# A gated-DeltaNet layer with SwiGLU: TensorE in order of emission in two phases, and transpositions in runs of eight

## The chip, the cores and the metric

One core of a Trainium2 chip runs the kernel. The metric is the device time of one execution in microseconds (us). TensorE is PE in the profile, and its weight loads are PEld; VectorE is DVE, ScalarE is ACT, GpSimd is POOL, and SyncE (SP) issues most of the transfers.

## The reference, cut to what matters

One decoder layer, 256 tokens wide, model width 2048, all in float32:

```python
mod = (silu(c) @ mod_w + mod_b)                  # 6 rows of 2048: sh1 sc1 ga1 sh2 sc2 ga2
h = x * (1 + sc1) + sh1
qkv, z, b, a = split(h @ w_in)                   # 2048 -> 8192 + 4096 + 64
qkv = silu(causal_depthwise_conv(qkv, conv_w))   # 4 taps
q, k = l2norm per head; beta = sigmoid(b); g = -exp(a_log) * softplus(a + dt_bias)
# chunked delta rule: (L + I) is unit lower triangular, L = strict(kb @ k.T) * decay
u, w = solve(L + I, [v * beta, kb * exp(gc)]); o, state = scan over chunks
y = (o * rsqrt(mean(o*o) + eps) * norm_w * silu(z)) @ w_out
x = layer_norm(ALPHA * x + (1 + ga1) * y)
h = x * (1 + sc2) + sh2
y = (silu(h @ w_gate) * (h @ w_up)) @ w_down     # 2048 -> 2 * 5632 -> 2048
out = layer_norm(ALPHA * x + (1 + ga2) * y)
```

## The kernel before, in words

Every weight matrix is streamed once in tiles of 128 x 1024 (`load_split`, L182 to L192: two tiles of 128 rows by 512 columns). ACT rounds a tile to `wh` (L190), and DVE takes the rest, `wl` (L191); a product of full precision is then three products, `wh` with the high half of the activations, `wl` with it, and `wh` with the low half (`Group.product`, L223 to L225). A `Group` makes 512 columns of output for both halves of the tokens: a chunk of 4 row blocks is 4 x 2 x 3 = 24 products of 512 columns, and one `wl` serves 12 of them. Four buffers each hold `raw`, `wh` and `wl`.

**The planner.** The program is unrolled by Python. `pos` counts chunks: one unit of position is 24 products. `Group.chunk` calls `advance(n + i/8)` ahead of every three products, and this runs each task that is due (`spawn(t, generator)`); a task that yields `d` goes on `d` units later. `at(p)` gives what is emitted a priority, the smaller the earlier. The order of each engine's instructions is then settled by the scheduler of the framework, engine by engine: from what is ready in its own model of time it takes the smallest priority. So positions decide priorities, and the order of TensorE is not that of the emission.

**Phase 1** (L924 to L935) makes the input projections for four groups of heads, `q` = 0 to 3, and the eight groups of the gate z (`z_group`). The groups of q = 0, and keys and queries of q = 1, are made ahead of it in parts. Behind a finished group come tasks. `conv_silu` (L457) turns two heads (`tr`, L462, four transpositions), convolves them on DVE (`cy`, L470, six a pair) and yields SILU units; then they are turned back (L494, L529). CONV is the distance of the first turn from its group. `gdn(q)` (L691) starts at some position s. Its four `la_task`s begin at s, s+0.5, s+1 and s+1.5 (LAGAP); each turns `dg` after LA1 (L547) and multiplies keys and queries after LA2 more (L556), and DVE writes `LA`. At s+3.0 `solve_task` (L564) is emitted, which inverts the 32 x 32 blocks on DVE: a transposition into `LD` (L573), 31 dependent pairs of `tmp` (L584) and `X` (L586), and a transposition into `XD` (L588). SOLVE = 5.4 units later (for q = 3 another ALONE = 1.5) TensorE's small products with `XD` follow (L600, L601), then four more steps, each HOP units on, and `state_task`. `gdn(q+1)` waits for the end of `gdn(q)`.

`mods_late` (L326) makes the rows ga1, sc2 and sh2 beside this: 32 loads a row, each with one accumulation `macc` on DVE (L272). At the end of half a row TensorE sums over partitions in four products (L351), ACT copies the sums (L277), and TensorE turns the copy (`to_columns`, L280) in the same step, with no yield between. Each of these float32 products stands twice in the trace.

**Phase 2** multiplies by `w_out` and takes the first layer norm; **phase 3** (L1046 to L1055) makes 11 gate and 11 up groups of 512 columns and then the down product. After an up group `act_task` turns 2 x 4 tiles of `an` = silu(gate) * up (L1039; `an` is L1031) and splits them (L814, L815); before, its two keys are due 0 and 0.5 units after the group's end. ga2's two halves are made in phase 3 as above, one `macc` every 2 units.

Of the kernel before, what the change touches and what calls it, by code (L numbers as in the profile page):

```python
# [2 lines left out]

# [6 lines left out]
F32R = mybir.dt.float32r  # L10
# [8 lines left out]
KT = D // 128  # L19
FF = 5632  # L20
FT = FF // 128
NQ = 4
# [7 lines left out]
def gdn_layer_kernel(ctx: ExitStack, tc: tile.TileContext, x, c, mod_w, mod_b, ln_g, ln_b,  # L30
# [3 lines left out]

    SPLIT, MOD0, MODEVERY = 10, 30.0, 0.95
    MGAP, CGAP0, CGAP, CSTEP = 1.5, 1.0, 2.0, 2.3
    CONV, PAIR, SILU = 0.2, 0.4, 2.4
    GDN, LAGAP, LA1, LA2, LA3, SOLVE, HOP = 3.0, 0.5, 0.3, 0.6, 1.5, 5.4, 0.6
    ALONE, MACW, ZW, OW = 1.5, 1.0, 0.1, 0.3


# [3 lines left out]
    held = ctx.enter_context(tc.tile_pool(name="held", bufs=1))  # L45
# [22 lines left out]
    def spawn(t, gen):  # L68
        heappush(tasks, (t, len(seq), gen))
        seq.append(gen)  # L70
# [3 lines left out]
    def drain(but=None):  # L74
        while any(x_[2] is not but for x_ in tasks):
            advance(now[0] + 0.1)

    def advance(t):
        now[0] = t
        while tasks and tasks[0][0] <= t:  # L80
            t0, i, gen = heappop(tasks)
            with at(t0):
                d = next(gen, None)
            if d is not None:
                heappush(tasks, (t0 + d, i, gen))
# [4 lines left out]
    def tp():  # L90
        return psum.tile([128, 512], F32, name="tp", tag="tp", bufs=2)
# [10 lines left out]
    w_in2 = w_in.rearrange("l k n -> (l k) n")  # L102
    w_out2 = w_out.rearrange("l k n -> (l k) n")
    w_gu2 = w_gu.rearrange("l k n -> (l k) n")
# [72 lines left out]
    pos = [0]  # L177
# [299 lines left out]
    def evac(t, ps):  # L477
        n = gp.tile([128, 512], F32, name="nat", tag="nat", bufs=4)
        act(n, ps, AF.Copy)
        return n  # L480
# [243 lines left out]
    def conv_start():  # L724
        t = max(now[0] + CONV, conv_free[0])
        conv_free[0] = t + CSTEP
        return t

    def qk_done(q, which):
        nat = []  # L730

        def done(t, ps, n=None):
            nat.append(evac(t, ps) if n is None else n)
            if t == 0:
                return
            both = []
            ss = work.tile([128, 2, 4], F32, name="ss", tag="ss", bufs=2)
            t1 = conv_start()
            for h in (0, 2):
                spawn(t1 + PAIR / 2 * h, qk_pair(q, which, nat, h, ss, both))  # L740
            spawn(t1 + PAIR + SILU + 0.6, qk_norm(q, which, ss, both))
        return done

    def v_done(q, half):
        nat = []

        def done(t, ps, n=None):
            nat.append(evac(t, ps) if n is None else n)
            if t == 0:
                return  # L750
            if q not in oq:
                oq[q] = held.tile([128, 2, 8, 128], F32, name=f"oq{q}", tag=f"o{q}")
            t1 = conv_start()
            for h in (0, 2):
                spawn(t1 + PAIR / 2 * h, v_pair(q, half, nat, h))
            if half == 1:
                spawn(t1 - CONV + GDN, gdn(q))
        return done
# [149 lines left out]
    def late_mods():  # L908
        yield from mods_late(ga1, 32, 1.0, MODEVERY)
        yield from mods_late(sc2, 64, 1.0, MODEVERY)  # L910
        yield from mods_late(sh2, 48, 0.0, MODEVERY)
        tt(A2, lng[:, 0:KT], sc2, op=OP.mult)
        tt(B2, lnb[:, 0:KT], sc2, op=OP.mult)
        tt(B2, B2, sh2, op=OP.add)
# [3 lines left out]
    mods_gen = late_mods()  # L918
    spawn(MOD0, mods_gen)

    def z_group(q, half):
        Group(w_in2, 8192 + q * 1024 + half * 512, h_hi, h_lo, KT, z_done(q, half)).run()

    for q in range(1, NQ):  # L924
        if q > 1:
            Group(w_in2, 2048 + q * 512, h_hi, h_lo, KT, qk_done(q, 0)).run()
            Group(w_in2, q * 512, h_hi, h_lo, KT, qk_done(q, 1)).run()
        for half in range(2):
            Group(w_in2, 4096 + q * 1024 + half * 512, h_hi, h_lo, KT, v_done(q, half)).run()
        if q == 1:  # L930
            z_group(0, 0)
    for z in range(1, 2 * NQ):
        z_group(z // 2, z % 2)
    z1 = pos[0]
    drain(mods_gen)  # L935

    with at(z1 - 2):
        r = [held.tile([128, D], F32, name=f"r{t}", tag=f"h{t}") for t in range(2)]
# [55 lines left out]
    NACT, NLATE = 13, 19  # L994
# [16 lines left out]
    late = {}  # L1011
# [7 lines left out]
    with tc.tile_pool(name="ph3", bufs=1, reuse_waits="tile") as p3:  # L1019
        def gate_done(j):  # L1020
            def done(t, ps):
                gates_[j, t] = p3.tile([128, 512], F32, name="sg", tag="sg", bufs=2)
                act(gates_[j, t], ps, AF.Silu)
            return done

        nats = {}

        def up_done(j):
            def done(t, ps):
                nats[j, t] = p3.tile([128, 512], F32, name="an", tag="an", bufs=6)  # L1030
                tt(nats[j, t], ps, gates_[j, t], op=OP.mult)  # L1031
            return done

        def act_task(key):
            j, i2 = divmod(key, 2)
            p = tp()
            for i in range(2):
                for t in range(2):
                    tr(p[:, i * 256 + t * 128:i * 256 + (t + 1) * 128],  # L1039
                       nats[j, t][:, (2 * i2 + i) * 128:(2 * i2 + i + 1) * 128], ident)  # L1040
            aT[key] = late[key] if key >= NACT else pair_tiles(p3, f"aT{key}")
            split_into(*aT[key], p)
            return
            yield

        for j in range(11):  # L1046
            Group(w_gu2, j * 512, h2_hi, h2_lo, KT, gate_done(j)).run(8 if j == 0 else 4, 8 if j == 0 else 4)
            Group(w_gu2, FF + j * 512, h2_hi, h2_lo, KT, up_done(j)).run()
            if j == 10:
                lt = [held.tile([128, 8, 256], F32R, name=f"lt{i}", tag=f"o{i}") for i in range(2)]  # L1050
                for i in range(22 - NLATE):
                    late[NLATE + i] = (lt[0][:, 2 * i:2 * i + 2, :], lt[1][:, 2 * i:2 * i + 2, :])
            for key in (2 * j, 2 * j + 1):
                if key < NLATE:
                    spawn(pos[0] + 0.5 * (key % 2), act_task(key))  # L1055
        drain()
        with at(pos[0]):
            for key in range(NLATE, 22):
                for _ in act_task(key):
                    pass  # L1060
        row2 = gate_row("h3", ga2, "ga2row")
        r2 = [held.tile([128, D], F32, name=f"rr{t}", tag=f"o{2 + t}") for t in range(2)]
        for t in range(2):
            nc.gpsimd.dma_start(r2[t], x1s[t])


        lrow = {}

        def finish(t):

            with at(now[0] - 40):
                mean, rstd, shift = norm_scalars(st2, t)

            shares = ((0, 0, 512, True), (1, 0, 512, True), (2, 0, 512, False), (3, 0, 512, False)) if t == 0 else (
                (0, 0, 512, True), (1, 0, 512, True), (3, 0, 512, False), (2, 0, 256, True), (2, 256, 512, False))
            for g, c0, c1, by_dve in shares:
                ot = r2[t][:, g * 512 + c0:g * 512 + c1]
                gamma, bias = (lrow[i, g][:, c0:c1] for i in range(2))
                if by_dve:
                    stt(ot, ot, mean, gamma, op0=OP.subtract, op1=OP.mult)  # L1080
                    stt(ot, ot, rstd, bias, op0=OP.mult, op1=OP.add)
                else:
                    act(ot, ot, AF.Identity, scale=rstd, bias=shift)
                    nc.gpsimd.tensor_tensor(ot, ot, gamma, op=OP.mult)
                    nc.gpsimd.tensor_tensor(ot, ot, bias, op=OP.add)
                nc.sync.dma_start(out2[t * 128:(t + 1) * 128, g * 512 + c0:g * 512 + c1], ot)

        def down_done(g):
            def done(t, ps):
                with at(now[0] - (40 if g == 3 else 0)):  # L1090
                    residual(row2, g, t, ps, r2, st2)
                if g == 3:
                    finish(t)
            return done

        for g in range(4):
            if g == 1:
                for i, src in enumerate((ln_g, ln_b)):
                    for gg in range(4):
                        tag, n = ("sg", 2) if i and gg > 1 else ("an", 6)  # L1100
                        lrow[i, gg] = p3.tile([128, 512], F32, name=f"l{i}{gg}", tag=tag, bufs=n)
                        nc.gpsimd.dma_start(lrow[i, gg], src[:, 1, gg * 512:(gg + 1) * 512].to_broadcast([128, 512]))
            Group(w_down2, g * 512, *pair_of(aT), FT, down_done(g)).run(8 if g == 3 else 4)
# [29 lines left out]
```

## Time and profile before

| | |
|---|---|
| median of 3 runs | 1722.5 us (1720.7 to 1725.71) |
| the profiled execution | 1725.16 us, of it 1723.4 us the span of its instructions |
| PE busy | 1668.0 us (97%), 8685 products |
| DVE busy | 1139.7 us (66%) |
| ACT busy | 882.0 us (51%) |
| HBM | 226 GB/s over the span |

Phase 1's groups stand from about 217 to 790 us, phase 2 to 967 us, the gate and up groups to 1470 us, and the down product to the end. PE's busy time is a union in which pipelined products overlap. So costs are read from starts: what separates the starts of two products beyond their usual distance is the cost of what stands between them.

### The profile page before, as it was taken

What the parts mean: (1) busy time and instruction counts of PE and PEld (TensorE: products, weight loads), DVE (VectorE), ACT (ScalarE), POOL (GpSimd) and SP (SyncE); (2) the same over time, 40 slices, a digit from 0 to 9 for tenths busy, and PEclk for the clock granted to TensorE, in tenths of its full rate; (3) what the DMA queues carried; (4) which work ended last, traced back from release to release, by engine and by line L of the source; (5) the groups of instructions that cost most, each with busy time, mean ns of one, the idle gap of its engine ahead of it and who ended that gap; (6) DMA issues with size and microseconds to landing.
All of it is one profiled execution on the core that took longest, in us unless ns stands there. A gap on an engine that the chain in (4) does not pass through costs nothing.

```text
span 1723.4 us, 23269 instructions
## 1 busy us (share of the span) xinstructions
PE 1668.0 (97%) x8685; PEld 1325.3 (77%) x8685; DVE 1139.7 (66%) x1635; ACT 882.0 (51%) x1430; POOL 61.2 (4%) x66
## 2 busy tenths in 40 slices
PE   5999999999999999999999999999999999999996
PEld 2666778787887878788787788888878887888885
DVE  2466988958966988847776865865467544455455
ACT  2433669769568667564333744444444443433332
POOL 0000000001001000000000000000000000000003
PEclk8999999999999999999999999999999999999998
DMA  9998786535864777747888586886678666756662
GB/s 347 364 338 286 223 283 191 170 112 159 255 204 117 241 251 241 245 147 238 302 278 282 158 270 185 304 268 189 189 246 284 191 185 207 249 192 192 196 193 101
DMA packets 184082, 390.82 MB, mean 227 GB/s; under 512 B 12112, under 2 KB 14592, under 8 KB 182944
## 3 DMA queue, kind: packets, MB, share of 16 engines
q1 hardware_dynamic: 181952, 378.64, 67.7%
q0 software_dynamic: 2016, 10.68, 1.8%
q8 instruction: 68, 1.11, 0.3%
q14 instruction: 46, 0.38, 0.1%
HBM read 385.08 MB, written 4.19 MB: 226 GB/s over the span
## 4 chain that ended last, share of the span: by engine, by line
PE 70%; DVE 12%; DMA 7%; ACT 5%; issue 4%; POOL 1%; SPq 1%; POOLq 0%; DVEq 0%; ACTq 0%
PE pj L223 19%; PE pj L225 19%; PE pj L224 19%; DMA mraw<-in_mod_w_dram 6%; DVE wl L191 5%; ACT wh L190 2%; PE gd L225 1%; PE gd L224 1%; DVE macc L272 1%; DVE cy L470 1%; PE gd L223 1%; DVE X L586 1%; DVE tmp L584 1%; PE tp L311 1%; PE tp L1039 1%
## 5 line engine op out<-in xcount | busy, mean ns | idle before, releaser
L191 DVE TENSOR_TENSOR wl<-raw,wh 128x1024 fp32r<-128x1024 f32 x522 | 635.1, 1222 | 376.7 <-ACT wh L190 374.1
L190 ACT ACTIVATE wh<-raw 128x1024 fp32r<-128x1024 f32 x522 | 552.3, 1061 | 602.4 <-PE pj L225 481.1
L223 PE MATMUL pj<-wh,h2T 128*128 128x512 f32 x704 | 278.2, 395 | 0.0
L225 PE MATMUL pj<-wh,h2T 128*128 128x512 f32 x704 | 276.7, 393 | 0.0
L224 PE MATMUL pj<-wl,h2T 128*128 128x512 f32 x704 | 276.5, 393 | 0.0
L223 PE MATMUL pj<-wh,hT 128*128 128x512 f32 x640 | 256.8, 403 | 0.0
L224 PE MATMUL pj<-wl,hT 128*128 128x512 f32 x640 | 256.5, 401 | 0.1
L225 PE MATMUL pj<-wh,hT 128*128 128x512 f32 x640 | 256.2, 401 | 0.0
L272 DVE SCALAR_TENSOR_TENSOR macc<-mraw,cond,macc 128x1024 f32<-128x1024 f32 x120 | 153.6, 1280 | 54.6 <-DMA mraw<-in_mod_w_dram 53.9
L223 PEld LDWEIGHTS pj<-wh,h2T 128*128 128x128 f32 x704 | 132.8, 189 | 30.5 <-issue 1.6
L225 PEld LDWEIGHTS pj<-wh,h2T 128*128 128x128 f32 x704 | 132.7, 189 | 28.7 <-issue 0.8
L224 PEld LDWEIGHTS pj<-wl,h2T 128*128 128x128 f32 x704 | 132.7, 188 | 27.8 <-issue 0.8
L223 PEld LDWEIGHTS pj<-wh,hT 128*128 128x128 f32 x640 | 120.8, 189 | 26.7 <-issue 3.3
L224 PEld LDWEIGHTS pj<-wl,hT 128*128 128x128 f32 x640 | 120.8, 189 | 24.5 <-DVE wl L191 0.9
L225 PEld LDWEIGHTS pj<-wh,hT 128*128 128x128 f32 x640 | 120.9, 189 | 24.4 <-issue 1.2
L470 DVE SCALAR_TENSOR_TENSOR cy<-tp,cw,cy 128x255 f32<-128x255 f32 (+2 forms) x192 | 86.2, 476 | 1.3 <-ACT cy L466 1.2
L224 PE MATMUL gd<-wl,hT 128*128 128x512 f32 x128 | 51.5, 404 | 1.4 <-DVE wl L191 1.4
L223 PE MATMUL gd<-wh,hT 128*128 128x512 f32 x128 | 49.9, 398 | 2.0 <-DVE part L256 1.1
L225 PE MATMUL gd<-wh,hT 128*128 128x512 f32 x128 | 51.8, 408 | 0.0
L311 PE MATMUL tp<-mraw,cond 128*32 128x256 f32 x368 | 34.9, 464 | 11.4 <-DMA mraw<-in_mod_w_dram 11.4
L223 PE MATMUL pj<-wh,oTc 128*128 128x512 f32 x112 | 43.9, 392 | 0.0
L225 PE MATMUL pj<-wh,oTc 128*128 128x512 f32 x112 | 43.8, 391 | 0.0
(388 smaller groups left out, 2266.3 us busy)
## 6 DMA issues: line engine op xcount, KB each, us to landing
raw<-in_gdn_w_in_dram SPq DMA_DIRECT2D x194, 512.0 KB, 4.6
mraw<-in_mod_w_dram SPq DMA_DIRECT2D x192, 512.0 KB, 5.4
raw<-in_ffn_w_gu_dram SPq DMA_DIRECT2D x176, 512.0 KB, 4.3
raw<-in_ffn_w_down_dram SPq DMA_DIRECT2D x88, 512.0 KB, 4.6
raw<-in_gdn_w_out_dram SPq DMA_DIRECT2D x64, 512.0 KB, 5.1
x<-in_x_dram SPq DMA_DIRECT2D x8, 256.0 KB, 5.9
r<-in_x_dram POOLq DMA_DIRECT2D x2, 1024.0 KB, 5.0
x1s<-r POOLq DMA_DIRECT2D x2, 1024.0 KB, 6.8
```

The costliest lines, as they stand in the source:

```text
L190: act(hi, raw, AF.Copy)
L191: tt(lo, raw, f32(hi), op=OP.subtract)
L223: mm(ps, sh, wh, start=start, stop=False)
L224: mm(ps, sh, wl, start=False, stop=False)
L225: mm(ps, sl, wh, start=False, stop=stop)
L272: return stt(acc, w, cond[:, k:k + 1], acc, op0=OP.mult, op1=OP.add)
L311: mm(p[32 * j:32 * j + 32, 0:hw], cond[:, k:k + 1].to_broadcast([128, 32]), raw[:, kl, j * hw:(j + 1) * hw], start=(k == 0), stop=(k == KT ...
L470: stt(y[:, o + s:o + 256], p[:, o:o + 256 - s], tap(3 - s, ct + i), y[:, o + s:o + 256], op0=OP.mult, op1=OP.add)
L584: tt(tv, LD[:, j + 1:32, j:j + 1].to_broadcast([128, n, m]), X[:, j, None, 0:m].to_broadcast([128, n, m]), op=OP.mult)
L586: tt(X[:, j + 1:32, 0:m], X[:, j + 1:32, 0:m], tv, op=OP.subtract)
L1039: tr(p[:, i * 256 + t * 128:i * 256 + (t + 1) * 128], nats[j, t][:, (2 * i2 + i) * 128:(2 * i2 + i + 1) * 128], ident)
```

## The change

It draws a chain through TensorE's instructions in two regions: inside `tc.manual_schedule(engines={PE})` TensorE issues what the region emits in the order of emission. The other engines' order stays the scheduler's, as does the place of instructions from outside a region. The regions are phase 1's groups from q = 1 to the last z group, with all that `advance` and `drain` run in them, and each j of the gate and up groups but j = 0. Three of the planner's constants change, and both keys of an up group are due 0.4 units after it, so that at the next eighth, 0.5, their eight transpositions are emitted in a row.

```diff
-    CONV, PAIR, SILU = 0.2, 0.4, 2.4
-    GDN, LAGAP, LA1, LA2, LA3, SOLVE, HOP = 3.0, 0.5, 0.3, 0.6, 1.5, 5.4, 0.6
+    CONV, PAIR, SILU = 0.45, 0.4, 2.4
+    GDN, LAGAP, LA1, LA2, LA3, SOLVE, HOP = 3.0, 0.5, 0.5, 0.6, 1.5, 5.4, 0.7
...
-    for q in range(1, NQ):
-        if q > 1:
-            Group(w_in2, 2048 + q * 512, h_hi, h_lo, KT, qk_done(q, 0)).run()
...
-    z1 = pos[0]
-    drain(mods_gen)
+    with tc.manual_schedule(engines={mybir.EngineType.PE}):
+        for q in range(1, NQ):
+            if q > 1:
+                Group(w_in2, 2048 + q * 512, h_hi, h_lo, KT, qk_done(q, 0)).run()
...
+        z1 = pos[0]
+        drain(mods_gen)
...
         for j in range(11):
-            Group(w_gu2, j * 512, h2_hi, h2_lo, KT, gate_done(j)).run(8 if j == 0 else 4, 8 if j == 0 else 4)
-            Group(w_gu2, FF + j * 512, h2_hi, h2_lo, KT, up_done(j)).run()
...
-                    spawn(pos[0] + 0.5 * (key % 2), act_task(key))
+            with tc.manual_schedule(engines={mybir.EngineType.PE}) if j else nullcontext():
+                Group(w_gu2, j * 512, h2_hi, h2_lo, KT, gate_done(j)).run(8 if j == 0 else 4, 8 if j == 0 else 4)
+                Group(w_gu2, FF + j * 512, h2_hi, h2_lo, KT, up_done(j)).run()
...
+                        spawn(pos[0] + 0.4, act_task(key))
```

The groups and their bodies are the same; what is left out of the diff is only indented.

## Rows read from the trace of the kernel before

**Rows 1.** The page, busy time (us, share of the span, instructions)

```profile
PE 1668.0 (97%) x8685; PEld 1325.3 (77%) x8685; DVE 1139.7 (66%) x1635; ACT 882.0 (51%) x1430; POOL 61.2 (4%) x66
```

**Rows 2.** Stretches of the four solves: length, PE, PEld, DVE, ACT, POOL busy, clock, DMA

```profile
304.00:352.00 48.00, 47.59 (x230) 38.03 (x232) 46.16 (x123) 33.40 (x72) 3.27 (x2) 1.00 0.57 166
417.00:485.00 68.00, 67.35 (x318) 54.18 (x317) 65.65 (x139) 42.12 (x81) 2.61 (x1) 1.00 0.80 252
548.00:609.00 61.00, 59.55 (x286) 47.69 (x285) 59.04 (x131) 39.19 (x76) 1.64 (x1) 1.00 0.71 223
676.00:725.00 49.00, 47.31 (x217) 38.82 (x215) 47.57 (x102) 23.15 (x26) 0.00 (x0) 1.00 0.81 260
```

**Rows 3.** Groups on DVE from 417.4 to 485.2 us: count, busy us, mean ns, idle before

```profile
L191 DVE TENSOR_TENSOR wl<-raw,wh 128x1024 fp32r<-128x1024 f32 x22 | 26.7, 1218 | 0.2 <-ACT wh L190 0.2
L470 DVE SCALAR_TENSOR_TENSOR cy<-tp,cw,cy 128x255 f32<-128x255 f32 (+2 forms) x36 | 17.1, 475 | 0.0
L272 DVE SCALAR_TENSOR_TENSOR macc<-mraw,cond,macc 128x1024 f32<-128x1024 f32 x12 | 15.3, 1274 | 0.4 <-DMA mraw<-in_mod_w_dram 0.4
L586 DVE TENSOR_TENSOR X<-X,tmp 128x126 f32<-128x126 f32 (+22 forms) x31 | 7.7, 249 | 0.0
L584 DVE TENSOR_TENSOR tmp<-LD,X 128x126 f32<-128x126 f32 (+22 forms) x31 | 7.7, 248 | 0.0
```

**Rows 4.** Timeline of PE, last keys product and first solve product: start, length in us

```profile
411.20 1.13 PE L556 MATMUL gd<-kq 128*128 128x256 f32 x4
...
485.30 0.21 PE L600 MATMUL gd<-XD,LA 32*32 32x32 f32 x1 [0.20 <-DVE XD L588]
```

**Rows 5.** Timeline of PE, phase 3: products around the first eight transpositions

```profile
999.92 0.39 PE L223 MATMUL pj<-wh,h2T 128*128 128x512 f32 x1
...
1010.80 0.39 PE L223 MATMUL pj<-wh,h2T 128*128 128x512 f32 x1
...
1015.77 0.39 PE L225 MATMUL pj<-wh,h2T 128*128 128x512 f32 x1
```

**Rows 6.** Timeline of PE, a run of eight transpositions

```profile
1471.25 0.40 PE L224 MATMUL pj<-wl,aT1h 128*128 128x512 f32 x1
1471.49 1.04 PE L838 MATMUL tp<-ident,ga 128*128 128x128 f32 x8
...
1473.06 0.39 PE L225 MATMUL pj<-wh,aT1l 128*128 128x512 f32 x1
```

**Rows 7.** Timeline, an up group's last product and its second `an`

```profile
1055.22 0.39 PE L225 MATMUL pj<-wh,h2T 128*128 128x512 f32 x1
...
1056.52 0.68 DVE L1031 TENSOR_TENSOR an<-pj,sg 128x512 f32<-128x512 f32 x1
```

**Rows 8.** Timeline, sums over partitions in phase 3

```profile
1262.18 0.39 PE L225 MATMUL pj<-wh,h2T 128*128 128x512 f32 x1
...
1262.50 0.62 PE L351 MATMUL tp<-macc,upper 128*32 128x256 f32 x2
...
1266.31 0.39 PE L224 MATMUL pj<-wl,h2T 128*128 128x512 f32 x1
```

**Rows 9.** Timeline, sums over partitions in phase 2

```profile
951.31 0.39 PE L225 MATMUL pj<-wh,oTc 128*128 128x512 f32 x1
951.63 0.64 PE L351 MATMUL tp<-macc,upper 128*32 128x256 f32 x8
...
952.70 0.36 ACT L277 ACTIVATE sums<-tp 128x256 f32<-128x256 f32 x1
952.76 0.40 PE L225 MATMUL pj<-wh,oTc 128*128 128x512 f32 x1
```

**Rows 10.** Waits of PE from 286 to 795 us, two of the groups: total, times, longest

```profile
PE gd L600 <- DVE XD L588: 2.1, 3, 1.7
PE tp L351 <- DVE tmp L584: 1.4, 1, 1.4
```

**Rows 11.** The stretch of the lowest clock: columns as in rows 2

```profile
960.50:967.50 7.00, 5.96 (x16) 4.59 (x17) 7.00 (x19) 5.87 (x10) 0.56 (x1) 0.52 0.62 221
```

More of the change, by code (lines that the diff above doesn't have):

```diff
@@ L1 @@
-from contextlib import ExitStack, contextmanager
+from contextlib import ExitStack, contextmanager, nullcontext
 from heapq import heappop, heappush
@@ L922, in z_group @@
         Group(w_in2, 8192 + q * 1024 + half * 512, h_hi, h_lo, KT, z_done(q, half)).run()
-    for q in range(1, NQ):
-        if q > 1:
-            Group(w_in2, 2048 + q * 512, h_hi, h_lo, KT, qk_done(q, 0)).run()
[L927 to L933, printed above, removed]
-    z1 = pos[0]
-    drain(mods_gen)
+    with tc.manual_schedule(engines={mybir.EngineType.PE}):
+        for q in range(1, NQ):
+            if q > 1:
+                Group(w_in2, 2048 + q * 512, h_hi, h_lo, KT, qk_done(q, 0)).run()
+                Group(w_in2, q * 512, h_hi, h_lo, KT, qk_done(q, 1)).run()
+            for half in range(2):
+                Group(w_in2, 4096 + q * 1024 + half * 512, h_hi, h_lo, KT, v_done(q, half)).run()
+            if q == 1:
+                z_group(0, 0)
+        for z in range(1, 2 * NQ):
+            z_group(z // 2, z % 2)
+        z1 = pos[0]
+        drain(mods_gen)
     with at(z1 - 2):
@@ L1046, in gdn_layer_kernel @@
         for j in range(11):
-            Group(w_gu2, j * 512, h2_hi, h2_lo, KT, gate_done(j)).run(8 if j == 0 else 4, 8 if j == 0 else 4)
-            Group(w_gu2, FF + j * 512, h2_hi, h2_lo, KT, up_done(j)).run()
[L1049 to L1054, printed above, removed]
-                    spawn(pos[0] + 0.5 * (key % 2), act_task(key))
+            with tc.manual_schedule(engines={mybir.EngineType.PE}) if j else nullcontext():
+                Group(w_gu2, j * 512, h2_hi, h2_lo, KT, gate_done(j)).run(8 if j == 0 else 4, 8 if j == 0 else 4)
+                Group(w_gu2, FF + j * 512, h2_hi, h2_lo, KT, up_done(j)).run()
+                if j == 10:
+                    lt = [held.tile([128, 8, 256], F32R, name=f"lt{i}", tag=f"o{i}") for i in range(2)]
+                    for i in range(22 - NLATE):
+                        late[NLATE + i] = (lt[0][:, 2 * i:2 * i + 2, :], lt[1][:, 2 * i:2 * i + 2, :])
+                for key in (2 * j, 2 * j + 1):
+                    if key < NLATE:
+                        spawn(pos[0] + 0.4, act_task(key))
         drain()
```

## The prediction

> **What bounds the kernel now.** I read the page first: PE is busy in 97% of the span, DVE in 66% [rows 1]. So what counts is what stands on PE between two products, and whether PE waits. Then the timeline of PE for the price of a product: from 999.92 to 1010.80 us there are 48 steps [rows 5], 10.88 / 48 = 0.2267 us each, so one unit of position, 24 products, is 5.44 us. Then the stretches of the four solves: in each, DVE is busy for all but 1.4 to 2.4 us of 48, 68, 61 and 49 us [rows 2], while over the whole span a third of its time is free. In these stretches two engines are full, PE with products and DVE with the solve and all else that was ready. Last the waits: behind the solve PE waited 2.1 us in all [rows 10], because the scheduler put L600 only where `XD` was ready. The reader is to see that PE loses little by waits before, and that it doesn't because its order was free.
>
> **Phase 3, transpositions.** Before, eight of them come as one, three and four single ones: from 1010.80 to 1015.77 us there are 17 steps of products [rows 5], 4.97 - 17 x 0.2267 = 1.12 us above their pace. A run of eight, from 1471.25 to 1473.06 us with 4 steps [rows 6], costs 1.81 - 0.91 = 0.90 us. Nine groups turn eight (the tenth only four): 9 x 0.22 = 2.0 us less. Is the run in time? It follows 12 products after the group's last, 13 x 0.2267 = 2.9 us after that one's start. The second `an` ended 1.98 us after that start, though DVE held it behind a `wl` [rows 7]. So I cost no wait; the cover is 0.9 us, less than one more `wl` (1.22 us [rows 3]) ahead of `an`. If that came each time, it would cost some 0.3 us a group, 3 us in all, and every product behind the run would wait too. PSUM, ACT and the transfers see the same work.
>
> **Sums over partitions.** In phase 3 the four products of L351 stand singly between products: from 1262.18 to 1266.31 us with 5 steps, 4.13 - 1.13 = 3.0 us [rows 8]. In one piece they cost 1.45 - 3 x 0.2267 = 0.77 us [rows 9]. Two halves lie in regions of phase 3: 2 x 2.2 = 4.5 us less. But L280 is emitted in the same step as L351, and it needs ACT's copy. In rows 9 the next product could start at about 952.2 us, and the copy ended at 953.06 us [rows 9]. In order of emission PE stands for that time, 0.9 us, and for 1.1 us more where a `wh` is ahead on ACT (as long as a `wl`, by rows 3, less a little). Queued behind L280 are all products. Six halves lie in regions (four in phase 1, two in phase 3): 5 to 12 us more; I take 1.1 us each, +6.6 us, near the lower end, since ACT is busy in about half of the span [rows 1].
>
> **The solve.** This decides. The last product of keys for a `gdn` that starts at s is emitted at s + 1.5 + LA1 + LA2 = s + 2.6, and L600 at s + 3.0 + 5.4 = s + 8.4: 5.8 units, 139 products, 31.6 us. With L556 itself (0.7 us) and eight fours of transpositions between them at half of 0.90 us, PE gets there after some 36 us; for q = 3, with ALONE and no convolutions, after 40. Before, it took 485.30 - 411.20 = 74 us for q = 1 [rows 4], because L600 floated to where `XD` was ready. In a chain it can't float, and all products stand behind it.
>
> How long does DVE need? For q = 1 the solve's first transposition starts at 417.4 us, 6 us after L556 [rows 3, 4], so 30 us of PE's time are left. The five groups of rows 3 sum to 74.5 us of busy time in 67.8 us, a factor of 0.91. In 30 us, less 3.6 us of transpositions, PE uses 26.4 / 0.2267 / 12 = 9.7 `wl` and not 22: 13.6 us saved. If `macc` and `cy` shrink with the time, 12 to 6 and 36 to 24, that saves 7.0 and 5.2 us. `XD` then comes after 42 us: a wait of **12 us**. By the same rates the other stretches [rows 2], of 48, 61 and 49 us, give 11, 10 and 9 us: 42 us for the four. Bounds: with nothing beside the solve and its `wl` on DVE, (15.4 + 3 + 11.8) x 0.91 = 27.5 us, no wait; with everything that filled the stretches before but the `wl` saved, 66 us. I take 28 us, two thirds of the middle count: the solve is emitted ahead of half of the convolutions, so some of them come after it, but rows 3 show that its 62 dependent steps were filled with whatever was ready. What is late next is the rest of the `gdn` chain, with the solves of the next q behind it.
>
> **The clock.** The granted clock fell to 0.52 in 960.5 to 967.5 us [rows 11], half of full speed, 1.2 GHz, behind waits of some us in which PE had little to do: 3.4 us of work lost. With waits of 10 us I expect this once or twice: +5 us (0 to 14). The Trainium skill, "TensorE: Matmul & The Clock Gate", section "HAM oscillation", has it that waits between bursts of products throttle the clock anew; by that rule each of the four waits pays it and the term would be 4 x 3.4 = 14 us. The row agrees on the fall; nothing before shows it for a wait inside phase 1.
>
> **Waits that go.** With longer CONV, LA1 and HOP, work that PE waits for should be ready. The two largest groups of waits between 286 and 795 us are 2.1 and 1.4 us [rows 10]; if the first is counted above, both vanish at best: -3.5 us. A chain can add waits at each hop instead; HOP is now 0.7 x 5.44 = 3.8 us, against a `wl` or a `wh` in front of a small copy. I set this at 0, between -2 and +15 us. L280 included, each new wait holds the products, and with them `raw` buffers and SP's queue of loads; 97% of PE leaves nothing to catch up with.
>
> **The sum**, against the profiled execution's 1725.2 us: -2.0 - 4.5 + 6.6 + 28 + 5 - 3.5 = +29.6, 1754.8 us. That execution was 2.7 us above the median, so the forecast is **1752 us**.
>
> **Rivals.** (1) *The chain costs nothing, faster.* One mechanism: DVE delivers `XD` within PE's 36 us, because a PE that starts less other work early leaves DVE to the solve. For it: the bound above without other work, 27.5 us; DVE's free third. Against: the stretches were full to 2 us in all four [rows 2]. It decides where `XD` comes under 36 us after the last L556. Then 1722.5 - 2.0 - 4.5 - 3.5 = 1712 us, with the sums' waits also absent, and 1719 us with them; at the best, if the smaller waits and single transpositions of phase 1 go too, 1708. (2) *No difference.* The solve's waits sum to 5 us or less and the sums' waits eat the gains of phase 3: 1722.5 - 10 + 6.6 + 3 = 1722 us. (3) *All fillers stay.* 66 us of waits at the solves, the clock lost at each: 1722.5 + 66 + 14 + 6.6 - 10 = 1799 us; halfway to it from the forecast, 1775 us. (4) *It doesn't do what it says*: the scheduler's order was the emission's already. Rows 8 and rows 5 exclude it, since single products of one step stand apart.
>
> **Numbers.** A measurement of this kernel can tell about 0.3%, 5.2 us. Chances: the forecast's case, slower by 6 to 50 us, 0.53; rival 3, 0.12; rival 1, 0.26; rival 2, 0.09. Faster 0.26, same 0.09, slower 0.65. The range from 1709 to 1775 us leaves out the upper half of rival 3 and the edge of rival 1; the likeliest case's own range is 1728 to 1772 us.
>
> **What would show it.** Right: PE waits at L600 for `XD` of 5 to 15 us each, at fewer products after L556 than before; L280 waits for ACT's copy; L351 in one piece; runs of eight at 0.9 us in phase 3; the stretches of the solves shorter than rows 2, DVE full in them. Wrong: no wait over 3 us at L600, and phase 1 as long as before or shorter; or `an` awaited in phase 3.

## The result, and the profile after

The median of 4 runs is 1870.0 us (1866.1 to 1870.8) against 1723.4 us of the kernel before on the same chip: a ratio of 1.0847 with an interval of 1.0824 to 1.0869, 147 us slower. The forecast, 1752 us, had the direction, and the time lies far outside its range.

The page of after, busy time and the granted clock in 40 slices, against [rows 1], and below it the clock of before:

```profile
PE 1696.2 (91%) x8685; PEld 1355.1 (73%) x8685; DVE 1149.8 (62%) x1635; ACT 888.3 (48%) x1432; POOL 59.5 (3%) x66
...
PEclk8999888898899889989999999999999999999998
```
```profile
PEclk8999999999999999999999999999999999999998
```

The same 8685 products stand in a span that is 144.4 us longer, DVE's share falls with PE's, and the clock falls below that of before in the left half alone. To find the stage, both traces are cut at the same products of L223 to L225: the 576th, 2304th, 3072nd, 5184th and 6240th. The stretches of before, then of after (length, PE, PEld, DVE, ACT, POOL busy, clock, DMA share, GB/s):

```profile
217.50:765.60 548.10, 538.31 (x3396) 434.01 (x3395) 432.49 (x860) 392.44 (x853) 28.75 (x23) 1.00 0.64 200
765.60:957.60 192.00, 188.71 (x870) 151.85 (x868) 140.89 (x157) 81.56 (x96) 4.95 (x3) 1.00 0.78 266
957.60:1464.20 506.60, 503.23 (x2238) 407.94 (x2236) 303.20 (x312) 225.91 (x257) 3.87 (x7) 0.99 0.72 225
```
```profile
223.60:920.70 697.10, 577.27 (x3447) 465.18 (x3446) 455.25 (x889) 411.20 (x885) 29.95 (x24) 0.91 0.51 156
920.70:1107.30 186.60, 183.88 (x825) 148.33 (x824) 129.61 (x131) 74.36 (x77) 2.04 (x2) 1.00 0.79 271
1107.30:1608.70 501.40, 495.80 (x2238) 408.63 (x2237) 301.86 (x312) 223.73 (x257) 3.86 (x7) 1.00 0.72 228
```

Phase 1 (first row of each) takes 149.0 us more. Ahead of it 6.1 us are lost; phase 2 gains 5.4 us, the gate and up groups (third row) 5.2 us. The down product has 242.8 us in both. So phase 3 did about what was forecast, and phase 1 decides.

What PE waits for in phase 1 of after, the largest groups (us in total, times, longest; [rows 10] are two of before):

```profile
PE gd L600 <- DVE XD L588: 57.2, 4, 23.9
PE tp L445 <- DVE q L443: 11.0, 1, 11.0
PE gd L670 <- DVE oq L666: 7.5, 4, 2.4
PE gd L547 <- ACT dg L543: 7.3, 6, 1.9
PE tp L494 <- DVE X L586: 4.7, 1, 4.7
PE gd L556 <- ACT dm L551: 4.3, 4, 1.7
...
PE tp L280 <- ACT sums L277: 3.0, 2, 2.5
PE tp L280 <- DVE X L586: 2.2, 1, 2.2
```

All groups of the view sum to 119.7 us; before, over the same products, to 9.4 us. Of the 119.7 us, 57.2 are the four solves, 5.2 the sums (L280), and 57.3 lie in some twenty groups of other hops, where PE had waited 7.1 us as long as the scheduler chose the order.

The solve itself. On PE's timeline of after, the last L556 and the first L600 of q = 2, where [rows 4] have q = 1 of before:

```profile
598.68 0.81 PE L556 MATMUL gd<-kq 128*128 128x256 f32 x3
...
662.84 0.26 PE L600 MATMUL gd<-XD,LA 32*32 32x32 f32 x1 [23.85 <-DVE XD L588]
```

Between the two stand 138 products (139 were planned); before, 228 to 283. The stretches from DVE's `LD` to its `XD`, as [rows 2]:

```profile
318.30:357.60 39.30, 26.72 (x115) 20.86 (x114) 35.18 (x100) 18.16 (x42) 1.64 (x1) 0.87 0.42 122
458.00:510.80 52.80, 34.01 (x150) 27.23 (x148) 47.51 (x106) 19.81 (x43) 1.64 (x1) 0.82 0.72 226
609.00:662.80 53.80, 27.77 (x130) 22.02 (x128) 48.98 (x111) 19.78 (x39) 1.64 (x1) 0.79 0.72 221
757.30:801.50 44.20, 34.44 (x159) 27.62 (x157) 42.19 (x100) 17.64 (x19) 0.00 (x0) 0.96 0.72 227
```

They are shorter than before (39 to 54 us against 48 to 68), since fewer products ask for fewer `wl`; but DVE is still busy for about nine tenths of each, and PE is not. What fills DVE, from q = 1's last L556 to its L600, and then in the 88 us up to q = 2's last L556 (count, busy us, mean ns, idle before):

```profile
L272 DVE SCALAR_TENSOR_TENSOR macc<-mraw,cond,macc 128x1024 f32<-128x1024 f32 x13 | 16.6, 1279 | 1.5 <-DMA mraw<-in_mod_w_dram 1.5
L191 DVE TENSOR_TENSOR wl<-raw,wh 128x1024 fp32r<-128x1024 f32 x12 | 14.6, 1217 | 1.4 <-ACT wh L190 1.4
L470 DVE SCALAR_TENSOR_TENSOR cy<-tp,cw,cy 128x255 f32<-128x255 f32 (+2 forms) x12 | 5.7, 472 | 0.0
```
```profile
L191 DVE TENSOR_TENSOR wl<-raw,wh 128x1024 fp32r<-128x1024 f32 x16 | 19.6, 1223 | 25.4 <-ACT wh L190 25.3
...
L272 DVE SCALAR_TENSOR_TENSOR macc<-mraw,cond,macc 128x1024 f32<-128x1024 f32 x2 | 2.5, 1264 | 0.6 <-DMA mraw<-in_mod_w_dram 0.6
```

This is the fault in one picture. In the solve, where DVE is what everybody waits for, stand 13 `macc`; in the following 88 us, where DVE is busy for 42.1 us, stand 2. By the planner's distance (MODEVERY, one `macc` every 0.95 units) it would be 6 and 9. DVE's order is still the scheduler's, PE's is the emission's, and the two disagree on where there is time. What starts the crowd stands on PE: `macc` has one buffer, so the first accumulation of a half (L271) follows L351, which reads the half before it.

```profile
453.48 0.64 PE L351 MATMUL tp<-macc,upper 128*32 128x256 f32 x8
...
454.39 0.75 DVE L271 TENSOR_SCALAR macc<-mraw,cond 128x1024 f32<-128x1024 f32 x1
```

The chain has L351 3.9 us behind q = 1's last L556. The half's 16 accumulations then stand from 454.4 to 514.6 us, and the next ones only from 618.4 us on, behind the next L351 at 615.6 us, again in a solve. In before L351 stands ahead of q = 1's solve too (412.3 us), but its half lasts until 496 us. No run moved L351 or gave `macc` a second buffer, so what that alone would give stays open.

The products, too, are dealt the wrong way round: 141 in q = 1's solve and 198 in the stretch behind it, against 283 and 128 before.

The clock, in the stretch behind a small wait (columns as above), around the end of q = 2's long one, and PE's timeline in the first of them:

```profile
456.10:462.90 6.80, 6.29 (x17) 5.03 (x18) 5.94 (x16) 1.48 (x3) 0.53 (x1) 0.51 0.62 222
...
657.80:667.80 10.00, 4.96 (x71) 4.26 (x72) 7.20 (x15) 4.36 (x7) 0.00 (x0) 0.50 0.60 173
```
```profile
456.61 1.01 PE L280 MATMUL tp<-ident,sums 128*128 128x4 f32 x4 [2.48 <-ACT sums L277]
...
461.89 0.63 PE L224 MATMUL pj<-wl,hT 128*128 128x512 f32 x1
462.32 0.63 PE L225 MATMUL pj<-wh,hT 128*128 128x512 f32 x1
```

A wait of 2.48 us at L280 is followed by 12 products whose starts lie 0.43 us apart and not 0.23: half of full speed, 1.2 GHz, and another 2.4 us. Counted on the timeline, neighbouring products of phase 1 with nothing between them start over 0.39 us apart in 112 places after and in 28 before: (112 - 28) x 0.2 = 17 us. This is a lower figure, since some of these steps are 0.57 or 0.79 us: added up above 0.2267 us each, all steps of this kind lost 40.7 us after and 17.5 us before, 23 us more. Behind the four waits at L600 stand 37 of the 112 places.

Phase 3, a run of eight and a half's sums, against [rows 5, 6] and [rows 8, 9]:

```profile
1295.79 0.39 PE L225 MATMUL pj<-wh,h2T 128*128 128x512 f32 x1
1296.02 1.03 PE L1041 MATMUL tp<-ident,an 128*128 128x128 f32 x8
1296.81 0.48 PE L223 MATMUL pj<-wh,h2T 128*128 128x512 f32 x1
...
1595.61 0.39 PE L225 MATMUL pj<-wh,h2T 128*128 128x512 f32 x1
1595.93 0.64 PE L351 MATMUL tp<-macc,upper 128*32 128x256 f32 x8
1597.41 0.61 PE L280 MATMUL tp<-ident,sums 128*128 128x4 f32 x4 [0.85 <-ACT sums L277]
1597.88 0.48 PE L223 MATMUL pj<-wh,h2T 128*128 128x512 f32 x1
```

From product to product, the run costs 1.02 - 0.23 us there and 0.1 us more at the next product, 0.89 us, as forecast. The sums cost 1597.88 - 1595.61 - 0.23 = 2.0 us and again 0.1 us behind, of which 0.85 us is the wait for ACT.

### The profile page after: what moved, and what is told of

It is laid out like the page before. It is cut to its first block, busy times and chain, and to the rows that moved or that the text cites. A ratio compares the mean times of both kernels' runs of the same rounds, so it can differ in the third digit from the quotient of the medians.

```text
span 1867.8 us, 23249 instructions
## 1 busy us (share of the span) xinstructions
PE 1696.2 (91%) x8685; PEld 1355.1 (73%) x8685; DVE 1149.8 (62%) x1635; ACT 888.3 (48%) x1432; POOL 59.5 (3%) x66
## 4 chain that ended last, share of the span: by engine, by line
PE 65%; DVE 13%; DMA 8%; ACT 6%; issue 6%; POOL 1%; SPq 1%; POOLq 0%; DVEq 0%; ACTq 0%
PE pj L223 18%; PE pj L224 18%; PE pj L225 18%; DMA mraw<-in_mod_w_dram 7%; DVE wl L191 5%; ACT wh L190 2%; DVE macc L272 2%; DVE cy L470 1%; PE gd L225 1%; PE gd L224 1%; PE gd L223 1%; DVE X L586 1%; PE tp L311 1%; DVE tmp L584 1%; PE gd L556 1%
## 5 line engine op out<-in xcount | busy, mean ns | idle before, releaser
L223 PE MATMUL pj<-wh,hT 128*128 128x512 f32 x640 | 277.0, 435 | 0.0
L223 PE MATMUL pj<-wh,h2T 128*128 128x512 f32 x704 | 275.7, 392 | 0.0
L225 PE MATMUL pj<-wh,h2T 128*128 128x512 f32 x704 | 275.0, 391 | 0.1
L225 PE MATMUL pj<-wh,hT 128*128 128x512 f32 x640 | 258.4, 404 | 0.0
L225 PEld LDWEIGHTS pj<-wh,h2T 128*128 128x128 f32 x704 | 132.6, 188 | 28.2 <-DVE h2T L979 0.7
L223 PEld LDWEIGHTS pj<-wh,h2T 128*128 128x128 f32 x704 | 132.6, 188 | 27.4 <-ACT h2T L974 0.4
L225 PEld LDWEIGHTS pj<-wh,hT 128*128 128x128 f32 x640 | 125.6, 196 | 29.5 <-issue 0.8
L223 PEld LDWEIGHTS pj<-wh,hT 128*128 128x128 f32 x640 | 126.9, 199 | 25.6 <-issue 2.5
L224 PEld LDWEIGHTS pj<-wl,hT 128*128 128x128 f32 x640 | 126.9, 198 | 23.8 <-DVE wl L191 0.9
L470 DVE SCALAR_TENSOR_TENSOR cy<-tp,cw,cy 128x255 f32<-128x255 f32 (+2 forms) x192 | 82.1, 474 | 6.5 <-ACT cy L466 6.5
L600 PE MATMUL gd<-XD,LA 32*32 32x32 f32 x128 | 7.6, 236 | 57.2 <-DVE XD L588 57.2
L223 PE MATMUL gd<-wh,hT 128*128 128x512 f32 x128 | 50.9, 406 | 2.7 <-DVE part L256 1.8
L225 PE MATMUL gd<-wh,hT 128*128 128x512 f32 x128 | 52.7, 414 | 0.0
L600 PEld LDWEIGHTS gd<-XD,LA 32*32 32x32 f32 x128 | 7.1, 151 | 58.9 <-DVE XD L588 49.0
```

What stands on the lines that cost most here:

```text
L223: mm(ps, sh, wh, start=start, stop=False)
L224: mm(ps, sh, wl, start=False, stop=False)
L225: mm(ps, sl, wh, start=False, stop=stop)
L470: stt(y[:, o + s:o + 256], p[:, o:o + 256 - s], tap(3 - s, ct + i), y[:, o + s:o + 256], op0=OP.mult, op1=OP.add)
L600: mm(ppv[32:64, s, :], la[0:32, s, 0, 32:64], XD[0:32, s, :], start=True, stop=True)
```

## The experiments

Each run was timed beside the kernel before on its own chip, so ratios are compared, not times. The stages, by the same products as above, in the profiled execution of each (us):

| run | ratio (95%) | to phase 1 | phase 1 | phase 2 | gate, up |
|---|---|---|---|---|---|
| before | 1 | 217.5 | 548.1 | 192.0 | 506.6 |
| after | 1.0847 (1.0824 to 1.0869) | 223.6 | 697.1 | 186.6 | 501.4 |
| phase 3 only | 0.9962 (0.9948 to 0.9977) | 218.3 | 548.4 | 193.7 | 503.3 |
| no chains | 1.0098 (1.0074 to 1.0121) | 223.3 | 565.1 | 189.1 | 503.6 |
| solve later | 1.0804 (1.0776 to 1.0831) | 222.3 | 650.6 | 229.2 | 501.6 |
| no `macc` | 1.0526 (1.0502 to 1.0551) | 217.6 | 655.1 | 187.4 | 501.2 |
| old distances | 1.0742 (1.0707 to 1.0778) | 216.9 | 682.3 | 186.7 | 500.9 |
| moved products | 1.0718 (1.0688 to 1.0748) | 224.1 | 673.1 | 190.5 | 502.9 |
| gates' PSUM | 1.0776 (1.0744 to 1.0809) | 222.2 | 682.8 | 187.5 | 502.5 |
| filled waits | 1.0834 (1.0803 to 1.0865) | 223.1 | 693.0 | 185.6 | 501.5 |
| priorities only | 1.0091 (1.0062 to 1.0121) | 217.9 | 551.9 | 198.9 | 507.0 |
| sums apart | 1.0062 (1.0039 to 1.0086) | 217.6 | 553.1 | 199.3 | 505.3 |
| phase 3, 0.3 units | 0.9984 (0.9970 to 0.9997) | 217.4 | 553.2 | 186.8 | 507.5 |
| phase 3, ga2 alone | 0.9957 (0.9940 to 0.9974) | 219.4 | 545.7 | 193.9 | 497.9 |

### Parts of the change

**Phase 3 only.** Phase 1 keeps the scheduler's order and the old constants.

```diff
-    with tc.manual_schedule(engines={mybir.EngineType.PE}):
+    with nullcontext():
         for q in range(1, NQ):
...
-    CONV, PAIR, SILU = 0.45, 0.4, 2.4
-    GDN, LAGAP, LA1, LA2, LA3, SOLVE, HOP = 3.0, 0.5, 0.5, 0.6, 1.5, 5.4, 0.7
+    CONV, PAIR, SILU = 0.2, 0.4, 2.4
+    GDN, LAGAP, LA1, LA2, LA3, SOLVE, HOP = 3.0, 0.5, 0.3, 0.6, 1.5, 5.4, 0.6
```

> The chain and the runs of eight in phase 3 alone; phase 1's order is free again and its three constants are the old ones. Theory (order of emission costs only where the planner's distances are shorter than what DVE and ACT need; in phase 3 they are long enough): phase 3 keeps what it has in the changed kernel, 5 us less than before, so about 1718 us. Rival (a chain costs wherever it stands): slower than 1723 us.

1720.8 us: 6.5 us faster by the ratio, as expected. The half of the change in phase 3 is good by itself, and beats both kernels.

**No chains.** The new constants and the new due times, with both regions opened to the scheduler.

```diff
-    with tc.manual_schedule(engines={mybir.EngineType.PE}):
+    with nullcontext():
...
-            with tc.manual_schedule(engines={mybir.EngineType.PE}) if j else nullcontext():
+            with nullcontext():
```

> The new constants and due times, but no chain in either phase. Theory: with the order free, positions only set priorities, so within 0.5% of the kernel before (1715 to 1732 us). Rival (the new distances CONV, LA1 and HOP make the tasks late, and the chain is innocent): over 1760 us.

1.0098, a miss: the constants that I had credited with 3.5 us less cost 17 us without any chain. With the distances longer, the `gdn` chain and what feeds it come later: the first L600 starts 4.4 us later than before (356.4 us), the last 14.6 us (739.6 us). 5.8 us are lost ahead of phase 1 and 17.0 us in it.

**Old distances.** The change with both chains and the old constants (the second half of the first diff of this section).

> The changed kernel with the three old constants (CONV 0.2, LA1 0.3, HOP 0.6), both chains kept. Theory (in a chain, PE stands wherever a distance is shorter than what ACT and DVE need): shorter distances, more waits at the turns and hops, 1870 to 1900 us. Rival (the new constants cost in a chain what they cost without one, 17 us in the run without chains): about 1853 us.

1.0742, the rival's time. In the chain, too, the constants cost (1.0847 - 1.0742) x 1723 = 18 us. PE's largest waits in its phase 1:

```profile
PE gd L600 <- DVE XD L588: 47.2, 4, 20.4
PE gd L547 <- ACT dg L543: 15.0, 9, 5.0
PE tp L445 <- DVE q L443: 11.5, 1, 11.5
```

A shorter LA1 doubles the waits for `dg` (15.0 against 7.3 us), and yet the kernel is faster than after. As I read it, a longer distance saves its own wait and delays all that hangs on it. The first L600 starts 18.1 us earlier than in after (339.5 us), the last 22.3 us (779.4 us), so most is gained ahead of the first solve; the three constants were not taken apart.

### What the solves' waits cost

**Solve later.** Products are put where DVE needs time: SOLVE = 8.0, so 201 products stand in each solve instead of 138.

```diff
-    GDN, LAGAP, LA1, LA2, LA3, SOLVE, HOP = 3.0, 0.5, 0.5, 0.6, 1.5, 5.4, 0.7
+    GDN, LAGAP, LA1, LA2, LA3, SOLVE, HOP = 3.0, 0.5, 0.5, 0.6, 1.5, 8.0, 0.7
```

> The changed kernel with SOLVE 8.0 and not 5.4: each L600 is emitted 2.6 units, 62 products or 14.1 us, later. Theory (the solves' waits are a distance that is too short): PE's waits at L600 fall from 57 to about 15 us, the clock falls less often, and the time is 1815 to 1835 us, though the chain of the four solves now ends about one unit behind phase 1's last product. Rival (DVE has too little time in all, so the waits only move): L600 waits less, other places more, and the time stays above 1855 us.

The waits at L600 fell from 57.2 to 7.8 us and phase 1 by 46.5 us, as the theory had it. Phase 2 took 42.6 us more, and the whole gained only (1.0847 - 1.0804) x 1723 = 7 us. The last product of `state_task` came at 891 us on PE's timeline, behind the last one of phase 1 (872.9), and phase 2 needs what it makes: its first product starts at 892.7 us. The stretch from 875 to 910 us, of after and then of this run:

```profile
875.00:910.00 35.00, 34.36 (x170) 28.08 (x170) 23.44 (x31) 19.46 (x23) 0.61 (x1) 1.00 0.56 166
```
```profile
875.00:910.00 35.00, 23.03 (x98) 17.71 (x99) 25.46 (x46) 11.29 (x36) 2.93 (x1) 0.76 0.64 220
```

PE is idle for 12 us where after had products; 6.2 us of it L225 waits for `oTa`, the last state's output. So the `gdn` chain has a length of its own, four solves and their hops, one after the other; a wait taken from PE by letting the solve start its products later comes back at the chain's end.

**No `macc`.** Of the 16 accumulations of each half of ga1, sc2 and sh2 all but the first are left out, so that these rows are made from one of 16 blocks; the loads stay.

```diff
-            ins = mac(acc, ahead.pop(0), k)
+            raw_ = ahead.pop(0)
+            if k == 0 or pin:
+                ins = mac(acc, raw_, k)
```

> The changed kernel without 15 of 16 accumulations of ga1, sc2 and sh2 on DVE (their loads stay; the rows' values are left out). In the changed kernel 12, 12 and 5 of these stood in the last three solves, 15, 15 and 6 us of DVE's time. Theory (DVE's other work in a solve is what makes it late): the waits at L600 fall from 57 to 20 to 28 us and the time to 1810 to 1835 us. Rival (the solve's own chain of dependent steps is the length, fillers cost it nothing): L600 still waits 45 us or more, time above 1850 us.

1817.7 us. The waits for `XD` fell to 21.8 us, and the time by (1.0847 - 1.0526) x 1723 = 55 us:

```profile
PE gd L602 <- DVE XD L590: 21.8, 4, 10.7
PE gd L672 <- DVE oq L668: 7.5, 4, 2.4
PE tp L447 <- DVE q L445: 7.3, 1, 7.3
```

The solves' stretches on DVE fell to between 36 and 41 us (39 to 54 in after). This shows what the rows of q = 1 above only suggest: the `macc` among the solve's steps make 35 of the 57 us that PE waits there. The solve of q = 0, which had none, makes PE wait 5.9 us as before; the others fell from 18.0, 23.9 and 9.4 us to 3.6, 10.7 and 1.6 us. Not all of the 55 us is theirs: 6.0 us are gained ahead of phase 1, and the wait of L445 (here L447) falls from 11.0 to 7.3 us. Without `macc` 21.8 us and the hops remain.

**Moved products.** All four stretches of a q are dealt anew: more to the solve, less to the hops.

```diff
-    GDN, LAGAP, LA1, LA2, LA3, SOLVE, HOP = 3.0, 0.5, 0.5, 0.6, 1.5, 5.4, 0.7
-    ALONE, MACW, ZW, OW = 1.5, 1.0, 0.1, 0.3
+    GDN, LAGAP, LA1, LA2, LA3, SOLVE, HOP = 3.0, 0.35, 0.3, 0.4, 1.2, 8.6, 0.4
+    ALONE, MACW, ZW, OW = 0.0, 1.0, 0.1, 0.3
```

> The changed kernel with products moved, in the order of emission, from the stretch between a solve's end and the next keys products (there 201 stand, and DVE is half idle) into the solves: SOLVE 8.6, and HOP 0.4, LA1 0.3, LA2 0.4, LAGAP 0.35, LA3 1.2, ALONE 0. Theory (the loss is that the emission deals the products to the wrong stretches): the cycle of one q falls from about 150 to 125 to 135 us, the waits at L600 to under 15 us in all, and the last state ends by about 820 us; the hops wait a little more; time 1770 to 1820 us. Rival (a fixed order loses the same whatever the distances): above 1850 us, as with SOLVE 8.0 alone.

1.0718, a miss: by the ratio 1847 us, close to the rival's 1850 us. PE's largest waits in its phase 1:

```profile
PE gd L547 <- ACT dg L543: 17.4, 8, 5.4
PE gd L600 <- DVE XD L588: 15.7, 3, 9.4
PE tp L445 <- DVE q L443: 10.9, 1, 10.9
PE gd L608 <- ACT nP L603: 4.9, 2, 2.6
```

The solves' 57.2 us became 15.7 us, and the hops, now short, took part of it back: all other waits of phase 1 rose from 62 to 77 us, and phase 1 is 24.0 us shorter. No set of these distances that was tried serves both.

### What single hops and the clock cost

**Gates' PSUM.** The second largest wait, 11.0 us at L445, has a cause of its own. The gates are emitted ahead of the region. Their second tile comes from the two `tp` places, and a convolution's turn (L462) that is emitted behind it (not in front of it, as the expectation has it) can't go ahead of it; in the chain all products wait behind that turn. Here the tile takes a `gd` place.

```diff
-        p = tp()
+        p = gd()
         mm(p[:, 0:64], upper, q.rearrange("p a b -> p (a b)"), start=True, stop=True)
```

> The changed kernel, with the second PSUM tile of the gates (L444) taken from the other pair of PSUM buffers (gd instead of tp), so that the turns of the convolution that are emitted in front of it don't hold its place. Theory (a wait in the chain is paid whole by all products behind it): the wait of 11.0 us at L445 goes, and with it the stretch of half clock behind it (45 products at half clock in the 13.7 us from 238.1 us, some 9 us): 11 to 20 us less, 1850 to 1860 us. Rival (the wait is only the first place where TensorE meets a DVE that is late with the whole start of phase 1): it turns up at the next small product, and the time stays at 1865 us or more.

1.0776, (1.0847 - 1.0776) x 1723 = 12 us less than after: the theory's side, by 1 us outside its range in the median (1860.8 us). The wait at L445 is 1.8 us, and the 324 products from the 576th on take 129.3 us instead of 138.1. L462 now starts at 224.5 us and L445 at 248.1 us; in after L462 follows L445, at 237.8 and 236.9 us. The next places don't take the wait over: this hop was worth its whole wait, 9.2 us, and the 3 us beyond are less than the intervals can tell.

**Filled waits.** PE gets products to do in the two longest waits, so that only the clock changes. Their results are overwritten.

```diff
-        ppv = gd().rearrange("p (s c) -> p s c", s=16)
+        fill = gd()
+        if q in (1, 2):
+            for i in range(75 if q == 1 else 100):
+                mm(fill, h_hi(0, 0), hT[0, 0][:, 0:2, :].rearrange("p a b -> p (a b)"), start=True, stop=True)
+        ppv = fill.rearrange("p (s c) -> p s c", s=16)
```

> The changed kernel with added products: 75 of 512 columns ahead of the first L600 of q = 1 and 100 ahead of that of q = 2, whose results are overwritten. They take 17 and 21 to 23 us at full clock, about as long as the two longest waits of TensorE (18.0 and 23.9 us), so TensorE is busy while it would wait. Theory (the clock is a cost of its own beside the waits: 38 and 37 products at half clock in the stretches that begin at 507.8 and 654.5 us, 0.2133 us each): the products themselves cost nothing, the half clock there goes, and the time falls by some 10 to 18 us, to 1852 to 1860 us. Rival (behind a wait TensorE is ahead of DVE again, and the half clock is absorbed in the next waits): no change or longer, 1866 to 1876 us.

1.0834 against 1.0847, the rival's side: no difference that the intervals can tell; the profiled execution is 5.5 us shorter. The waits at the solves fell by 39.5 us, to 17.7 us, and behind both filled ones the clock is full; the stretch behind q = 2's:

```profile
658.10:679.30 21.20, 21.15 (x289) 17.55 (x290) 9.12 (x8) 15.62 (x28) 2.10 (x3) 1.00 0.59 190
```

The theory was priced wrongly before it was tested. In this expectation and in that of the gates I had placed the stretches of half clock 10.6 us too late against the products (I had read their times without taking off the start of the span), and counted 38 and 37 products (45 there), most of which start 0.23 us apart. Placed rightly there are 11 and 7, worth 18 x 0.2 = 3.6 us, which fits a gain between none and 5.5 us. So the clock behind the two long waits is the small part of the 17 to 23 us; the larger part lies elsewhere.

### Phase 3 by other means

**Priorities only.** No chain anywhere; the eight transpositions and L351 get a priority 40 units earlier, and both keys are due 0.4 units after the group.

```diff
-            p = tp()
-            for i in range(2):
+            with at(now[0] - 40):
+                p = tp()
+                for i in range(2):
...
```

> The kernel before, no chain anywhere; both keys of an up group are due at 0.4, and the eight transpositions and the four products L351 get a priority 40 units earlier, so that the scheduler takes them in a row. Theory (phase 3's gain is that of whole runs, and a chain is only one way to them): runs of eight and L351 in one piece, also in phase 2, and L280 free to wait: 8 to 10 us less than before, ratio 0.995. Rival (the gain needs the chain, since the scheduler deals single products between anyway): within 2 us of before.

1.0091, slower, a miss. From 760 us on the two largest waits are these:

```profile
PE tp L352 <- DVE macc L272: 7.7, 2, 4.4
PE tp L1041 <- DVE an L1032: 5.9, 3, 2.9
```

As I read it, an early priority puts a product where the scheduler's model has its operand ready; the chip's DVE comes later, by up to 4.4 us here, and PE stands. The chain puts it where the emission does, 2.9 us behind the group's last product's start, and `an` is there or nearly: after's nine runs of eight cost 0.89 us in the median and 1.04 in the mean, 1.4 us more in all, of which the view shows 0.9 us as two waits for `an`.

**Sums apart**, the phase 3 of the first run with 0.3 units between ACT's copy and L280, and L351 with the early priority:

```diff
-                qv = to_columns(p, 256, 2)
+                act(sums, p[:, 0:256], AF.Copy)
+                yield 0.3
+                q = tp()
...
+                    mm(q[:, 4 * i:4 * i + 4], sums[:, i * 128:(i + 1) * 128], ident[:, 0:128:32], start=True, stop=True)
```

> The chain in phase 3 alone, and 0.3 units between ACT's copy of the sums and L280, so that products stand in between; L351 with an early priority where there is no chain. Theory: the run with phase 3's chain alone (ratio 0.9962) less the two waits of L280 (1.4 us each) and less 2.2 us for the half in phase 2: ratio 0.993 to 0.994. Rival (the wait at L280 was hidden): ratio 0.995 to 0.996.

1.0062, a miss, with 10.7 us of waits of L351 for `macc`, for the same reason.

**The same without the priority:**

> Phase 3's chain alone with the old constants (as in the run of phase 3 only), and between ACT's copy of the sums and TensorE's turning of it (L280) 0.3 units of position, so that in the chain some seven products stand between them. No priority is moved. Theory: the two waits at L280 in the regions of phase 3 (1.4 us each) go and nothing takes their place, phase 1 and 2 as before: a ratio of 0.994 to 0.996 against the kernel before. Rival (moving the sums' tail later shifts phase 1 and 2, as in the run with priorities): 0.998 or more.

0.9984, the rival's side. The priority had cost (1.0062 - 0.9984) x 1723 = 13 us. From the 3264th product on, the end of phase 3's first up group, the gate and up groups take 448.5 us, 2.8 less than in the run of phase 3 only, but PE comes there 4.1 us later: in phases 1 and 2, where the order is free, the 0.3 units only push the sums' end back.

**The 0.3 units in ga2 alone**, whose halves lie in phase 3; against the run before:

```diff
-                yield 0.3
+                if pin:
+                    yield 0.3
```

> As the run before of phase 3's chain with 0.3 units ahead of L280, but the 0.3 units only in ga2's two halves, which lie in the regions of phase 3; ga1, sc2 and sh2 are as in the kernel before. Theory (the 0.3 units were paid in phases 1 and 2, some 4 us up to the first products of phase 3, where the order was free): up to phase 3 as in the run of phase 3 only, the rest of gate and up groups 448 to 449 us, 1718 us, a ratio of 0.994 to 0.996 against the kernel before. Rival (what phase 3 saves at L280 it loses elsewhere): 0.997 or more.

0.9957, as the theory had it: 1718.4 us, the best of all the kernels here, though its interval overlaps that of phase 3 only. All that PE waits for from 957 us on is one line, which the kernel before has as well:

```profile
PE tp L976 <- DVE hf L984: 2.9, 1, 2.9
```

## Why the prediction was wrong

The forecast was 118 us too low. The two terms that were furthest off are the hops, set at 0 and measured at +50 us, and the solve, +28 us and measured at +55; then come the constants and the clock.

**What held.** The direction and its mechanism: in order of emission PE stands at L600 until `XD` is there, behind 138 to 141 products for q = 0 to 2 where 139 were worked out, in shorter stretches in which DVE is still busy for nine tenths. Phase 3: the excess of its transpositions over the pace of products fell by 1.4 us over the nine groups (2.0 forecast) and that of its sums by 2.6 us (4.5 - 2.2 forecast); a half's sums cost 2.17 us in the mean, 1.4 us more than the 0.77 of [rows 9], where 1.1 us was taken. The waits at L280 in the regions are 6.9 us (6.6 forecast). The cover of `an`, 0.9 us, was too short in two of the nine runs, at 1.4 us for both, under the 3 us named.

**The solve, +28 us, measured +55.** The middle count had 11, 12, 10 and 9 us; the waits were 5.9, 18.0, 23.9 and 9.4 us. Two steps failed, for q = 1 as follows. The first is "if `macc` and `cy` shrink with the time, 12 to 6". `cy` did, to 12 where 24 were counted, 5.7 us less, and the `wl` came out as counted (10 from `LD` to `XD`); `macc` did not, 13, some 7 x 1.28 = 9 us more than counted: the 16 of a half don't spread over the time, they crowd into the 60 us behind L351, which frees their buffer. The reason why I then took two thirds of the count, 28 of 42 us, that convolutions come after the solve, was about `cy` alone, and no row told where the scheduler would put the `macc` on DVE. The second step is the factor of 0.91, taken over from before: here the five groups of [rows 3] sum to 50.1 us and fill 52.8 us, a factor of 1.05. DVE was idle for 5.3 us of them, 2.4 us before. `XD` came 52.8 us behind the solve's start and not 42: some 4 us by the counts and 7 us by the factor. The run without `macc` takes 35 us of the four waits' 57 away. That the waits are not longer still is PE's doing: without them it needs 40 to 45 us from L556 to L600, and not 36 (40 for q = 3). The upper bound of 66 us held.

**The hops, 0, measured +50.** "A chain can add waits at each hop instead" stood in the text with an upper end of 15 us; waits came in some twenty groups of places. One alone (L445) was 11.0 us, and taking its cause away gave 12 us back. The bound was drawn from the distance HOP against one `wl`, as if each hop had a DVE or an ACT free but for one instruction; it left out hops whose producers wait in turn (L547 and L556 for ACT's `dg` and `dm`), the turns behind a PSUM place, and all hops of the convolutions.

**The clock, +5, measured 17 to 23** by the steps of products. Behind each of the four waits at L600 7 to 11 of these steps are at half clock, and most slow steps stand elsewhere, so the fall did not come once or twice. The Trainium skill, "TensorE: Matmul & The Clock Gate", section "HAM oscillation", has waits between bursts throttle the clock each time; the trace agrees, and the 14 us worked out by it were nearer than my 5 us. The nearness is in part luck: the four waits that I gave them to hold 37 of the 112 slow steps, some 7 us, and with two of them filled nothing measurable came back.

**Waits that go, -3.5, measured +17.** The constants by themselves cost 17 us in the scheduler's order and 18 us in the chain. I had looked at what each distance protects and not at the `gdn` chain that each lengthens.

These terms overlap and don't cover all. Of phase 1's 149.0 us, waits are 110.3 us (55.1 at L600, 5.0 at L280, 50.2 elsewhere) and the steps with nothing between two products 23 us. The last 16 us lie in steps with small products between them (without the waits 145.3 us above the pace, 129.6 before), which no run took apart.

**Rivals.** All fillers stay (1799 us) had the larger part of the solves' waits, 57 of 66 us, and was too low for the same reason as the forecast: it had no price for the hops.

## What to carry to other kernels

Fix an engine's order only where each operand is there well before its place, by rows: phase 3's `an` came 0.9 us ahead, and that half of the change gains 0.4%. Around a serial chain on another engine leave the order free, or price every hop of the chain as a wait that all products behind it pay, not only the one hop that looks longest; and a distance that protects one hop lengthens the chain that the next phase waits for. Before giving a stretch away, ask which engine is full in it: here the products were taken out of the solves, where DVE was the bound, and put where DVE was half idle. And look for what an instruction of the fixed engine sets free on another one: here 16 `macc` follow each L351.

## What the runs showed of the hardware

The length of a wait does not tell the clock that it costs: behind a wait of 2.48 us at L280 eleven steps of products were at 1.2 GHz, behind the waits of 5.9, 9.4, 18.0 and 23.9 us at L600 ten, nine, eleven and seven, after the 64 small products of L600 and L601. And the lost clock of the two longest waits hardly showed in the time when it was given back, while filling them with 175 products cost nothing that could be measured (1.0834 against 1.0847).
